# Loading and splitting the second half's up operands at other steps of the first half's down stage

## The chip, the cores and the metric

The kernel runs on one core of one Trainium2 chip. The metric is device time in microseconds (us) of one execution. The kernel before was timed in three runs; one further execution was recorded by the hardware profiler, and the trace comes from that one.

The engines are written as in the profile: PE (TensorE, matmuls; PEld its weight loads), DVE (VectorE), ACT (ScalarE), POOL (GpSimd) and SP (SyncE, which issues nearly all DMAs of this kernel). "SPq" is SyncE's issuing of transfers.

## The reference, cut to what matters

One decoder layer for 2048 tokens of width 1024, in f32: a token mixer of three groups of heads, then a channel mixer, then a final norm.

```python
D_MODEL = 1024; SEQ = 2048; DEPTH = 1
D_FF = 256 * ((8 * D_MODEL // 3 + 255) // 256)      # 2816

# channel mixer, in words of the reference's docstring:
#   Pre-RMSNorm with adaLN, then up-projection, causal depthwise conv (width 3),
#   SiLU-gated product, down-projection. Added to the residual with an adaLN gate.
# A final RMSNorm with gain is applied at the end.
```

The change lies in the channel mixer. Its up-projection (1024 to 2 x 2816) and its down-projection (2816 to 1024) are the two large matrix products behind the token mixer.

## The kernel before, in words

**Stages.** The token mixer comes first, in four blocks of 512 tokens. The channel mixer follows in two halves, s = 0 and s = 1, of 1024 tokens. Each half has an up stage and a down stage: up 0, down 0, up 1, down 1.

**How a product is computed.** Each large product is cut into 2 x 2 blocks and done with seven block products in place of eight (Strassen's scheme in Winograd's form); the products are numbered 1 to 7. Their operands are sums and differences of blocks. To keep f32 accuracy at the speed of a narrower type, every operand is split into a high and a low part: ScalarE casts the raw tile into the high part (L1186), VectorE subtracts that from the raw tile (L1187), and TensorE runs three matmuls per pair of operands: high x low and low x high around high x high (`split3`, L292 to L294). A split thus needs the raw tile in SBUF, then ScalarE, then VectorE, and TensorE waits for the second.

**The down stage** (L1633). The products run in the order TURN = 1, 2, 6, 7, 4, 5, 3. Each has 11 steps k, and each step has 12 matmuls of 128x512: four row tiles p, three matmuls each. Per step two raw tiles are loaded and split: `rd`, a weight block or a stored sum of weight blocks, into `dA`, and `rb`, an operand made from the up stage's outputs, into `dB`. Names are dA{half}_{product}_{step}. Products 1, 6, 7 and 4 add up in the same four PSUM banks `dX`; product 2 and product 5 have banks `dY`, and product 3 its own four banks, also called `dX`. After a product VectorE adds the banks, scaled by a gate, onto the residual rows `y` (L1672): the evacuation. Product 7's first matmuls wait until product 6 has been read out of the shared banks.

**Work woven into the down stage.** After each step of products 4, 5 and 3 the down stage calls `next(between)`, 33 calls in all. For the first half `between` is the generator `up_inputs(B)` (L1346), which prepares operands of the *second* half's up stage; each `yield` in it hands back to the down stage. It loads raw rows hr1_t_k (L1350) into a ring of three tiles (`t2m`, L1335) and works on them:

- Operands 1 and 2: the eight rows hr1_0_k "a" are loaded and split as they are.
- For k = 0 to 3 three "b" rows are loaded: b11 = hr1_0_k, b12 = hr1_1_k, b22 = hr1_1_(k+4). Three subtractions (L1360, L1363, L1367) make operands 5, 6 and 7 from them, each followed by a split into `B1_i_k` (in some tiles the high and low part are called `hB1`, `lB1`). After the second a copy of the difference is stored in DRAM (`t2d`, L1365), for `up_inputs_rest` (L1371), which makes operands 4 and 3 after the down stage.

In all that is 20 yields; what is left of the generator after the down stage would be run by the loop behind it.

**Behind it** come the weights for the second half's up stage: `up_weights` loads raw blocks and stored sums of blocks (`s`, loaded at L1401 into a ring of two tiles) and splits them into A1_f_i. The up stage's first matmuls also need the banks that product 3 used and a ScalarE copy `m` of an earlier result (L1474).

**What sets the order.** TensorE's order is written out by hand. The order on VectorE, ScalarE, SyncE and GpSimd is set by a scheduler when the program is built: it takes the instruction that is ready by its own estimate and has the highest priority. The down stage's loads and splits are raised by 60, its evacuations more; the generator's work is not raised. It is still put wherever the scheduler believes an engine free and the inputs there, which can be far ahead of the step at which it is written: the first "b" rows are written in product 4 and stand at the border between products 6 and 7. On the chip each engine then runs its list strictly in that order: an instruction that waits holds everything behind it on its engine. Two helpers touch the order: `marked(op)` (L251) remembers an instruction, and `pinned(fn)` (L255) issues what fn makes after the remembered one.

The order and reuse of tiles matter as well: a load into a ring's tile waits until the tile's last reader is done.

Of the kernel before, what the change touches and what calls it, by code (L numbers as in the profile page):

```python
# [14 lines left out]
ALU = mybir.AluOpType  # L15
# [109 lines left out]
def trunk(ctx, tc, xT, vecs, cvec, cst, rope, msk, wada, win, walow, wgla, wout, wup, wdown, out):  # L125
# [41 lines left out]
    V, S, G, T = nc.vector, nc.scalar, nc.gpsimd, nc.tensor  # L167
# [83 lines left out]
    def marked(op):  # L251

        mark[:] = [op.ins]

    def pinned(fn):  # L255

        with tc.issue_after(mark[0]):
            fn()
# [925 lines left out]
    def split(src, hi, lo):  # L1184

        S.copy(hi, src)  # L1186
        V.tensor_tensor(lo, src, hi, op=ALU.subtract)  # L1187
        return hi, lo

    def low_inputs(s, tile):  # L1190

        B = {}
        for i in (1, 2):
            for k in range(4):
                x = tile(f"hr{s}_{i}_{k}a")
                nc.sync.dma_start(x[:], h2d[2 * s, k + 4 * (i - 1)][:])
                B[i, k] = split(x[:], *hc_tile(f"B{s}_{i}_{k}"))
        return B

    def up_op(A, s, f, i, src):  # L1200
        t = w4_tile(f"A{s}_{f}_{i}")
        A[i] = split(src, t[:, 0:512], t[:, 512:1024])
# [45 lines left out]
    def split_made(B, i, raw):  # L1248
        for k, x in enumerate(raw):
            B[i, k] = split(x[:], *hc_tile(f"B0_{i}_{k}"))  # L1250
# [78 lines left out]
    def t2k(name):  # L1329
        return pg.tile([P, 512], F32, tag="t2k", name=name, bufs=4)  # L1330
# [4 lines left out]
    def t2m(name):  # L1335
        return pg.tile([P, 512], F32, tag="t2m", name=name, bufs=3)
# [6 lines left out]
    def up_op_in(B, i, k, src):  # L1343
        B[i, k] = split(src[:], *hc_tile(f"B1_{i}_{k}"))

    def up_inputs(B):  # L1346

        def raw(t, k, why):
            x = t2m(f"hr1_{t}_{k}{why}")
            nc.sync.dma_start(x[:], h2d[2 + t, k][:])  # L1350
            return x

        op = lambda i, k, src: up_op_in(B, i, k, src)
        for i in (1, 2):
            for k in range(4):
                op(i, k, raw(0, k + 4 * (i - 1), "a"))
                yield
        for k in range(4):
            b11, b12, b22 = raw(0, k, "b"), raw(1, k, "b"), raw(1, k + 4, "b")
            V.tensor_tensor(b11[:], b12[:], b11[:], op=ALU.subtract)  # L1360
            op(5, k, b11)
            yield
            V.tensor_tensor(b11[:], b22[:], b11[:], op=ALU.subtract)  # L1363
            op(6, k, b11)
            nc.sync.dma_start(t2d[k][:], b11[:])  # L1365
            yield
            V.tensor_tensor(b12[:], b22[:], b12[:], op=ALU.subtract)  # L1367
            op(7, k, b12)
            yield
# [325 lines left out]
    for k in range(4):  # L1695
        x = t2k(f"hr0_3_{k}")
# [5 lines left out]
    hc_room = R_H + R_T + R_A4 + R_HC  # L1702
    B = {}
    ahead = up_inputs(B)
    down_stage(0, ahead)
    A = up_weights(1, 0)
# [107 lines left out]
```

## Time and profile before

| | |
|---|---|
| three timed runs | 2415.09, 2420.59, 2421.57 us (median 2420.59) |
| the profiled execution | 2411.75 us, of which the span of the trace is 2410.0 |
| granted TensorE clock | 0.997 of full speed |
| DMA traffic | 525.78 MB, mean 218 GB/s over the span |
| first half's products 7, 4, 5 and 3 | 1636 to 1758 us of the span |
| one step of a product (12 matmuls) | 2.7 us |

The profile's page shows, for each engine, its busy time; then the chain of waits, followed back from the last instruction; then groups of instructions by line. Rows of the trace in order of time have the start in us, the duration, the engine, the line, the operation, output <- inputs and the shape; in square brackets stands the engine's idle time just before, and what ended it. Names are shown there without their numbers (`hr_0b` is hr1_0_0b, hr1_1_0b or hr1_1_4b), and several instructions in a row of one form are put together as "x3". A row of a transfer group has the median time from issue to landing at its end. A matmul is shown with 0.39 us where nothing holds it, but follows the one before by 0.23 us, since they are pipelined.

In a row of the view by stretches stand the stretch, its length, and for each engine (TensorE, its weight loads, VectorE, ScalarE, GpSimd, SyncE) the busy time and count of instructions in it; behind them the granted clock, the share in which the DMA engines were busy, and the GB/s that they moved.

### The profile page before, as it was taken

What the parts mean: (1) busy time and instruction counts of PE and PEld (TensorE: products, weight loads), DVE (VectorE), ACT (ScalarE), POOL (GpSimd) and SP (SyncE); (2) the same over time, 40 slices, a digit from 0 to 9 for tenths busy, and PEclk for the clock granted to TensorE, in tenths of its full rate; (3) what the DMA queues carried; (4) which work ended last, traced back from release to release, by engine and by line L of the source; (5) the groups of instructions that cost most, each with busy time, mean ns of one, the idle gap of its engine ahead of it and who ended that gap; (6) DMA issues with size and microseconds to landing.
All of it is one profiled execution on the core that took longest, in us unless ns stands there. A gap on an engine that the chain in (4) does not pass through costs nothing.

```text
span 2410.0 us, 51886 instructions
## 1 busy us (share of the span) xinstructions
PE 2365.0 (98%) x20523; PEld 1960.7 (81%) x20523; DVE 1817.1 (75%) x3391; ACT 1290.4 (54%) x2311; POOL 154.3 (6%) x275
## 2 busy tenths in 40 slices
PE   7999999999999999999999999999999999999998
PEld 5788878888788878887888888888878888888887
DVE  7687867868577746877988888866878787778566
ACT  4675456744665457644554454554455455555452
POOL 1000100000000100001000000000010100000000
PEclk9999999999999999999999999999999999999999
DMA  7655676897788857888554454686765444448663
GB/s 273 231 185 188 232 264 238 278 333 263 259 299 298 280 198 274 272 280 273 176 170 153 140 157 151 227 288 212 225 208 167 144 149 144 151 152 281 200 199 116
DMA packets 228885, 525.78 MB, mean 218 GB/s; under 512 B 25849, under 2 KB 28833, under 8 KB 228641
## 3 DMA queue, kind: packets, MB, share of 16 engines
q1 hardware_dynamic: 225440, 511.98, 63.7%
q0 software_dynamic: 3200, 10.49, 1.2%
q8 instruction: 161, 2.64, 0.4%
q14 instruction: 84, 0.68, 0.1%
HBM read 392.87 MB, written 129.50 MB: 217 GB/s over the span
## 4 chain that ended last, share of the span: by engine, by line
PE 77%; DVE 9%; DMA 6%; ACT 4%; issue 3%; SPq 0%; POOL 0%; DVEq 0%; ACTq 0%; POOLq 0%
PE X L292 6%; PE X L293 6%; PE X L294 6%; PE Z L293 3%; PE Z L294 3%; PE Z L292 3%; PE dX L292 3%; PE dX L294 3%; PE dX L293 3%; PE psqkvgr L292 3%; PE psqkvgr L294 2%; PE psqkvgr L293 2%; PE y L292 2%; PE y L293 2%; PE y L294 2%
## 5 line engine op out<-in xcount | busy, mean ns | idle before, releaser
L292 PE MATMUL X<-B,A 128*128 128x512 f32 x572 | 223.1, 390 | 0.7 <-ACT u L1490 0.7
L293 PE MATMUL X<-B,A 128*128 128x512 f32 x572 | 222.8, 390 | 0.3 <-DVE B L1187 0.3
L294 PE MATMUL X<-B,A 128*128 128x512 f32 x572 | 222.6, 389 | 0.0
L1187 DVE TENSOR_TENSOR dA<-rd,dA 128x512 fp32r<-128x512 f32 x154 | 106.0, 689 | 94.4 <-ACT dA L1186 93.9
L1186 ACT CAST dA<-rd 128x512 fp32r<-128x512 f32 x154 | 95.5, 621 | 149.3 <-PE dX L294 57.5
L292 PE MATMUL dX<-dB,dA 128*128 128x512 f32 x396 | 154.2, 389 | 1.0 <-DVE y L1672 1.0
L293 PE MATMUL dX<-dB,dA 128*128 128x512 f32 x396 | 154.2, 389 | 0.3 <-DVE dB L1187 0.3
L294 PE MATMUL dX<-dB,dA 128*128 128x512 f32 x396 | 154.1, 389 | 0.0
L1187 DVE TENSOR_TENSOR A<-s,A 128x512 fp32r<-128x512 f32 x176 | 120.5, 686 | 39.5 <-ACT A L1186 39.5
L1186 ACT CAST A<-s 128x512 fp32r<-128x512 f32 x176 | 108.5, 617 | 60.8 <-PE Z L294 41.9
L292 PE MATMUL psvgh<-hvgh,ha 128*128 128x256 f32 x480 | 139.6, 291 | 0.0
L293 PE MATMUL psvgh<-lvgh,ha 128*128 128x256 f32 x480 | 135.7, 283 | 0.0
L294 PE MATMUL psvgh<-hvgh,ha 128*128 128x256 f32 x480 | 135.7, 283 | 0.0
L292 PEld LDWEIGHTS X<-B,A 128*128 128x128 f32 x572 | 107.4, 188 | 23.9 <-ACT u L1490 1.7
L293 PEld LDWEIGHTS X<-B,A 128*128 128x128 f32 x572 | 107.4, 188 | 23.0 <-DVE B L1187 1.0
L294 PEld LDWEIGHTS X<-B,A 128*128 128x128 f32 x572 | 107.4, 188 | 22.3
L293 PE MATMUL Z<-B,A 128*128 128x512 f32 x308 | 120.5, 391 | 1.4 <-DVE B L1187 1.4
L292 PE MATMUL Z<-B,A 128*128 128x512 f32 x308 | 120.2, 390 | 0.3 <-ACT B L1186 0.2
L294 PE MATMUL Z<-B,A 128*128 128x512 f32 x308 | 119.9, 389 | 0.0
L1186 ACT CAST A<-r 128x512 fp32r<-128x512 f32 x132 | 82.3, 623 | 63.5 <-PE Z L294 60.0
L1187 DVE TENSOR_TENSOR A<-r,A 128x512 fp32r<-128x512 f32 x132 | 90.6, 687 | 30.3 <-ACT A L1186 29.9
L1187 DVE TENSOR_TENSOR dB<-rb,dB 128x512 fp32r<-128x512 f32 x154 | 105.4, 686 | 6.8 <-ACT dB L1186 6.8
(491 smaller groups left out, 6780.5 us busy)
## 6 DMA issues: line engine op xcount, KB each, us to landing
gs<-yv SPq DMA_DIRECT2D x154, 256.0 KB, 3.0
rb<-gs SPq DMA_DIRECT2D x154, 256.0 KB, 4.1
r<-wup SPq DMA_DIRECT2D x143, 256.0 KB, 3.4
s<-sumsu SPq DMA_DIRECT2D x132, 256.0 KB, 3.2
wada<-wada SPq DMA_DIRECT2D x48, 512.0 KB, 4.3
rd<-sumsd SPq DMA_DIRECT2D x88, 256.0 KB, 4.0
rd<-wdown SPq DMA_DIRECT2D x66, 256.0 KB, 4.0
x<-xT SPq DMA_DIRECT2D x64, 256.0 KB, 5.5
```

The source lines that it names most:

```text
L292: T.matmul(ps, lhs[0], rhs[0], start=first, stop=False, skip_group_check=more)
L293: T.matmul(ps, lhs[0], rhs[1], start=False, stop=False, skip_group_check=more)
L294: T.matmul(ps, lhs[1], rhs[0], start=False, stop=last, skip_group_check=more)
L1186: S.copy(hi, src)
L1187: V.tensor_tensor(lo, src, hi, op=ALU.subtract)
```

## The change

The generator `up_inputs` is written differently, and `split` marks its subtraction:

```diff
@@ -1184,7 +1184,7 @@
     def split(src, hi, lo):
 
         S.copy(hi, src)
-        V.tensor_tensor(lo, src, hi, op=ALU.subtract)
+        marked(V.tensor_tensor(lo, src, hi, op=ALU.subtract))
         return hi, lo
 
@@ -1353,11 +1353,14 @@
         op = lambda i, k, src: up_op_in(B, i, k, src)
         for i in (1, 2):
             for k in range(4):
-                op(i, k, raw(0, k + 4 * (i - 1), "a"))
+                x = raw(0, k + 4 * (i - 1), "a")
                 yield
+                op(i, k, x)
         for k in range(4):
             b11, b12, b22 = raw(0, k, "b"), raw(1, k, "b"), raw(1, k + 4, "b")
-            V.tensor_tensor(b11[:], b12[:], b11[:], op=ALU.subtract)
+            yield
+            yield
+            pinned(lambda: V.tensor_tensor(b11[:], b12[:], b11[:], op=ALU.subtract))
             op(5, k, b11)
             yield
             V.tensor_tensor(b11[:], b22[:], b11[:], op=ALU.subtract)
```

An "a" row is loaded, the down stage runs one step, and then the row is split. The three "b" rows of a k are loaded, two steps pass, and only then the first subtraction is written, tied behind the last marked one (the split that the down stage wrote last). The generator now has 28 yields; there are still 33 calls. Lines below it have moved by three.

The loads and matmuls are the same, and so is the arithmetic. TensorE's order does not change; on the other engines the built order differs in 42 rows (VectorE), 22 (ScalarE), 16 (SyncE) and 8 (GpSimd). The eight "a" rows move nowhere. Three places show the rest.

VectorE at the border between the first half's products 6 and 7, before:

```order
L1187 TENSOR_TENSOR dA0_7_5_20507<-rd0_7_5_20505,dA0_7_5_20507 128x512
L1187 TENSOR_TENSOR dB0_7_5_20512<-rb0_7_5_20510,dB0_7_5_20512 128x512
L1360 TENSOR_TENSOR hr1_0_0b_20879<-hr1_1_0b_20881,hr1_0_0b_20879 128x512
L1187 TENSOR_TENSOR lB1_5_0_20887<-hr1_0_0b_20879,hB1_5_0_20886 128x512
L1672 SCALAR_TENSOR_TENSOR y0_1_0_19865<-dX0_0_19612,mod_102,y0_1_0_19865 128x512
L1672 SCALAR_TENSOR_TENSOR y0_1_0_19865<-dX0_1_19613,mod_102,y0_1_0_19865 128x512
L1672 SCALAR_TENSOR_TENSOR y0_1_2_19866<-dX0_2_19614,mod_102,y0_1_2_19866 128x512
L1672 SCALAR_TENSOR_TENSOR y0_1_2_19866<-dX0_3_19615,mod_102,y0_1_2_19866 128x512
L1187 TENSOR_TENSOR dA0_7_6_20529<-rd0_7_6_20527,dA0_7_6_20529 128x512
```

and in the changed kernel:

```order
L1187 TENSOR_TENSOR dA0_7_5_20507<-rd0_7_5_20505,dA0_7_5_20507 128x512
L1187 TENSOR_TENSOR dB0_7_5_20512<-rb0_7_5_20510,dB0_7_5_20512 128x512
L1187 TENSOR_TENSOR dA0_7_6_20529<-rd0_7_6_20527,dA0_7_6_20529 128x512
L1675 SCALAR_TENSOR_TENSOR y0_1_0_19865<-dX0_0_19612,mod_102,y0_1_0_19865 128x512
L1675 SCALAR_TENSOR_TENSOR y0_1_0_19865<-dX0_1_19613,mod_102,y0_1_0_19865 128x512
L1675 SCALAR_TENSOR_TENSOR y0_1_2_19866<-dX0_2_19614,mod_102,y0_1_2_19866 128x512
L1675 SCALAR_TENSOR_TENSOR y0_1_2_19866<-dX0_3_19615,mod_102,y0_1_2_19866 128x512
L1187 TENSOR_TENSOR dB0_7_6_20534<-rb0_7_6_20532,dB0_7_6_20534 128x512
```

The first subtraction for k = 0 and the split of its result stood ahead of the evacuation of product 6; now one split of a weight for product 7 stands there. The other four operations of k = 0 came after the evacuation and are gone from there too.

VectorE between the first half's products 4 and 5, in the changed kernel; this is where k = 0 stands now:

```order
L1187 TENSOR_TENSOR dB0_4_10_20914<-rb0_4_10_20912,dB0_4_10_20914 128x512
L1363 TENSOR_TENSOR hr1_0_0b_20879<-hr1_1_0b_20881,hr1_0_0b_20879 128x512
L1370 TENSOR_TENSOR hr1_1_0b_20881<-hr1_1_4b_20883,hr1_1_0b_20881 128x512
L1187 TENSOR_TENSOR lB1_5_0_20931<-hr1_0_0b_20879,hB1_5_0_20930 128x512
L1187 TENSOR_TENSOR dA0_5_0_20957<-rd0_5_0_20955,dA0_5_0_20957 128x512
L1187 TENSOR_TENSOR dB0_5_0_20962<-rb0_5_0_20960,dB0_5_0_20962 128x512
L1366 TENSOR_TENSOR hr1_0_0b_20879<-hr1_1_4b_20883,hr1_0_0b_20879 128x512
L1187 TENSOR_TENSOR dA0_5_1_20985<-rd0_5_1_20983,dA0_5_1_20985 128x512
```

Before, dA and dB of product 5's step 0 followed dB0_4_10 directly. The loads of the three rows stay where they were in SyncE's list, at the border between products 6 and 7; the store of the difference (L1365 before, L1368 now) goes 28 operand loads later.

VectorE in product 3, the last of the first half, before (n3a and sqn3 are sums of squares for the final norm):

```order
L1363 TENSOR_TENSOR hr1_0_3b_21190<-hr1_1_7b_21194,hr1_0_3b_21190 128x512
L1533 SCALAR_TENSOR_TENSOR y0_0_2_19861<-y0_0_2_19861,vec2_15933,n3b0_0_20961 128x512
L1187 TENSOR_TENSOR dA0_3_5_21453<-rd0_3_5_21451,dA0_3_5_21453 128x512
L391 TENSOR_TENSOR n3a0_1_19617<-n3a0_1_19617,sqn3_0_1_5_21322 128x512
L1187 TENSOR_TENSOR B1_6_3_21231<-hr1_0_3b_21190,B1_6_3_21231 128x512
L1187 TENSOR_TENSOR B1_7_3_21260<-hr1_1_3b_21192,B1_7_3_21260 128x512
L391 TENSOR_TENSOR n3a0_1_19617<-n3a0_1_19617,sqn3_0_1_6_21325 128x512
L1187 TENSOR_TENSOR dB0_3_5_21458<-rb0_3_5_21456,dB0_3_5_21458 128x512
```

and where k = 3 stands in the changed kernel:

```order
L1187 TENSOR_TENSOR dB0_3_7_21502<-rb0_3_7_21500,dB0_3_7_21502 128x512
L1363 TENSOR_TENSOR hr1_0_3b_21366<-hr1_1_3b_21368,hr1_0_3b_21366 128x512
L1187 TENSOR_TENSOR dA0_3_8_21519<-rd0_3_8_21517,dA0_3_8_21519 128x512
L1187 TENSOR_TENSOR dB0_3_8_21524<-rb0_3_8_21522,dB0_3_8_21524 128x512
L1187 TENSOR_TENSOR B1_5_3_21417<-hr1_0_3b_21366,B1_5_3_21417 128x512
L1187 TENSOR_TENSOR dA0_3_9_21541<-rd0_3_9_21539,dA0_3_9_21541 128x512
L1187 TENSOR_TENSOR dB0_3_9_21546<-rb0_3_9_21544,dB0_3_9_21546 128x512
L1366 TENSOR_TENSOR hr1_0_3b_21366<-hr1_1_7b_21370,hr1_0_3b_21366 128x512
L1187 TENSOR_TENSOR dA0_3_10_21563<-rd0_3_10_21561,dA0_3_10_21563 128x512
L1187 TENSOR_TENSOR dB0_3_10_21568<-rb0_3_10_21566,dB0_3_10_21568 128x512
L1187 TENSOR_TENSOR B1_6_3_21443<-hr1_0_3b_21366,B1_6_3_21443 128x512
L1370 TENSOR_TENSOR hr1_1_3b_21368<-hr1_1_7b_21370,hr1_1_3b_21368 128x512
```

The six operations of k = 3 stood ahead of dB0_3_5 (step 5); now they begin behind dB0_3_7, and the last (the split B1_7_3) comes three rows after these, between the first splits A1_0_i of the second half's weights. In SyncE's list the loads of k = 3 move too. Before:

```order
L1365 DMA t2d2_15906<-hr1_0_2b_21105 128x512
L1350 DMA hr1_0_3b_21190<-h2d2_3_173 128x512
L1340 DMA rd0_3_7_21495<-sumsd7_11127 128x512
L1350 DMA hr1_1_3b_21192<-h2d3_3_181 128x512
L1350 DMA hr1_1_7b_21194<-h2d3_7_185 128x512
L1658 DMA rb0_3_7_21500<-gs0_3_7_215 128x512
```

and in the changed kernel:

```order
L1661 DMA rb0_3_8_21522<-gs0_3_8_216 128x512
L1350 DMA hr1_0_3b_21366<-h2d2_3_173 128x512
L1340 DMA rd0_3_9_21539<-sumsd9_13912 128x512
L1350 DMA hr1_1_3b_21368<-h2d3_3_181 128x512
L1661 DMA rb0_3_9_21544<-gs0_3_9_217 128x512
L1350 DMA hr1_1_7b_21370<-h2d3_7_185 128x512
L1340 DMA rd0_3_10_21561<-sumsd10_14966 128x512
```

They stood at the loads of step 7 and stand now at those of steps 8 to 10. The rows of k = 1 and k = 2 keep their place in SyncE's list; on VectorE k = 1 keeps its order, and k = 2 mixes differently with four splits.

## The prediction

> **What bounds the kernel now.** I read the page's engine shares first, then the chain of waits, then each engine's rows in time order for the stretch that the change touches.
>
> ```profile
> PE 2365.0 (98%) x20523; PEld 1960.7 (81%) x20523; DVE 1817.1 (75%) x3391; ACT 1290.4 (54%) x2311; POOL 154.3 (6%) x275
> PE 77%; DVE 9%; DMA 6%; ACT 4%; issue 3%; SPq 0%; POOL 0%; DVEq 0%; ACTq 0%; POOLq 0%
> ```
>
> TensorE is busy for 98% of the span and carries 77% of the chain. A change that leaves its matmuls alone can only open or close gaps between them, so the question is which gaps lie where the change works: the last products of the first half's down stage and the first products of the second half's up stage. The largest is at the border between down products 6 and 7 (each row gives start, duration, instruction, and in brackets the idle time before it and what ended it):
>
> ```profile
> 1634.96 0.39 PE L294 MATMUL dX<-dB,dA 128*128 128x512 f32 x1
> 1636.38 0.47 PE L292 MATMUL dX<-dB,dA 128*128 128x512 f32 x1 [1.03 <-DVE y L1672]
> 1636.68 0.40 PE L293 MATMUL dX<-dB,dA 128*128 128x512 f32 x1
> ...
> 1666.18 0.39 PE L294 MATMUL dX<-dB,dA 128*128 128x512 f32 x1
> 1666.41 0.39 PE L292 MATMUL dX<-dB,dA 128*128 128x512 f32 x1
> ```
>
> Unhindered, matmuls start 0.23 us apart, as at the next border (7 to 4, 1666.18 to 1666.41). At the border 6 to 7 it is 1636.38 - 1634.96 = 1.42, and 0.30 for the next one: 1.19 + 0.07, about 1.26 us lost. Product 7 adds onto the banks of product 6, so it waits until VectorE has taken product 6 out of them (L1672). That evacuation was late:
>
> ```profile
> 1631.21 0.69 DVE L1187 TENSOR_TENSOR dB<-rb,dB 128x512 fp32r<-128x512 f32 x1
> 1633.50 0.69 DVE L1360 TENSOR_TENSOR hr_0b<-hr_0b,hr_0b 128x512 f32<-128x512 f32 x1 [1.59 <-DMA hr_0b<-h2d]
> 1634.88 0.69 DVE L1187 TENSOR_TENSOR lB<-hr_0b,hB 128x512 fp32r<-128x512 f32 x1 [0.69 <-ACT hB L1186]
> 1635.48 2.06 DVE L1672 SCALAR_TENSOR_TENSOR y<-dX,mod,y 128x512 f32<-128x512 f32 x3
> ...
> 1665.15 2.72 DVE L1672 SCALAR_TENSOR_TENSOR y<-dX,mod,y 128x512 f32<-128x512 f32 x4
> ```
>
> VectorE stood 1.59 us at the first subtraction for the second half (L1360) until its rows had landed, then 0.69 us for ScalarE's cast, and only then evacuated, from 1635.48. At the next border, with no such work in its queue, it began at 1665.15, 1.26 us ahead of the matmul that needs it. The two rows were asked for shortly before:
>
> ```profile
> 1627.57 0.90 SPq L1350 DMA_DIRECT2D hr_0b<-h2d  x2
> ...
> hr_0b<-h2d SPq DMA_DIRECT2D x2, 256.0 KB, 5.2
> ```
>
> Issued from 1627.57, they took 5.2 us to land; VectorE was free at 1631.9.
>
> **The change part by part.** *The eight rows of operands 1 and 2:* the text loads them one step earlier, but in the built order neither their transfers nor their splits move on any engine. 0 us.
>
> *Row k = 0.* Its subtraction and split leave the place ahead of the evacuation and go behind the split of product 4's last operand; its loads stay. Ahead of the evacuation now stands one weight split of product 7 (dA of step 6), whose cast needs a buffer that TensorE frees once per step:
>
> ```profile
> 1627.27 0.62 ACT L1186 CAST dA<-rd 128x512 fp32r<-128x512 f32 x1
> 1629.95 0.62 ACT L1186 CAST dA<-rd 128x512 fp32r<-128x512 f32 x1 [0.57 <-PE dX L294]
> 1634.22 0.62 ACT L1186 CAST hB<-hr_0b 128x512 fp32r<-128x512 f32 x1 [3.13 <-DVE hr_0b L1360]
> ```
>
> The rhythm is 2.7 us, so without the 3.13 us wait the next cast falls at 1632.7, its subtraction at 1633.3 to 1634.0, and the evacuation has read the first bank by 1634.7; TensorE wants that bank at 1634.96 + 0.23 = 1635.2. The gap closes with 0.5 us to spare. **-1.26 us.**
>
> The Trainium skill, SBUF — State Buffer, section The DMA setup-cost knee, fits a transfer by 2 us plus its bytes at 436 GB/s, an estimate of 2.6 us for 256 KB; by it the rows would have been down before VectorE was free, there would be no wait of 1.59 us, and this term would be near 0 (rival 3 has the chance of that); the row has 5.2, twice as much.
>
> At the new place VectorE has this room:
>
> ```profile
> 1676.03 0.69 DVE L1187 TENSOR_TENSOR dB<-rb,dB 128x512 fp32r<-128x512 f32 x1
> 1678.14 0.69 DVE L1187 TENSOR_TENSOR dA<-rd,dA 128x512 fp32r<-128x512 f32 x1 [1.42 <-ACT dA L1186]
> 1680.86 0.69 DVE L1187 TENSOR_TENSOR dA<-rd,dA 128x512 fp32r<-128x512 f32 x1 [1.43 <-ACT dA L1186]
> ```
>
> Six operations of k = 0 (three subtractions, three splits, 0.6 us apart) are 3.6 us against 1.4 us idle in each 2.7 us step: absorbed in three steps. Their rows landed 40 us before. What queues behind them is splits for product 5, which TensorE reaches 30 us after 1666.41, at 1696: 18 us of cover for at most 3.6 us of lateness, and 3.6 us would be the price without it. The three casts go to ScalarE, which waits for TensorE's buffers there. The store of the difference moves 28 operand loads back in SP's queue and is read only in the second half. 0 us.
>
> *Rows k = 1 and 2* keep their loads' place in SP's queue; k = 1 keeps its order on VectorE, k = 2 only mixes differently with four splits. 0 us.
>
> *Row k = 3* can go either way. In product 3 VectorE has little lead, and one split comes late:
>
> ```profile
> 1727.07 0.69 DVE L1360 TENSOR_TENSOR hr_3b<-hr_3b,hr_3b 128x512 f32<-128x512 f32 x1 [1.53 <-DMA hr_3b<-h2d]
> 1738.89 0.69 DVE L391 TENSOR_TENSOR n3a<-n3a,sqn 128x512 f32<-128x512 f32 x1 [1.59 <-ACT sqn L390]
> 1741.31 0.68 DVE L1187 TENSOR_TENSOR dB<-rb,dB 128x512 fp32r<-128x512 f32 x1
> ...
> 1737.09 0.62 ACT L1186 CAST dA<-rd 128x512 fp32r<-128x512 f32 x1 [3.90 <-DMA rd<-sumsd]
> ...
> 1741.37 0.39 PE L292 MATMUL dX<-dB,dA 128*128 128x512 f32 x1
> 1742.05 0.50 PE L293 MATMUL dX<-dB,dA 128*128 128x512 f32 x1 [0.29 <-DVE dB L1187]
> ```
>
> TensorE loses 0.68 - 0.23 = 0.45 us and about 0.11 in the restart, 0.56. In the new order the six operations of k = 3 and the 1.53 us wait leave the place ahead of this dB (step 5) and stand behind step 7. What still holds dB is ScalarE, which must pass the cast at 1737.09 (3.90 us on a transfer) before the square that VectorE adds first. So I put dB at about 1738.4, 3 us in time. **-0.56 us.**
>
> Late next is the same work, now between product 3 and the second half's first weights:
>
> ```profile
> 1750.77 0.69 DVE L1187 TENSOR_TENSOR A<-r,A 128x512 fp32r<-128x512 f32 x1 [0.59 <-ACT A L1186]
> 1751.81 0.69 DVE L1187 TENSOR_TENSOR A<-r,A 128x512 fp32r<-128x512 f32 x1 [0.35 <-ACT A L1186]
> 1752.42 1.29 DVE L1187 TENSOR_TENSOR A<-s,A 128x512 fp32r<-128x512 f32 x2
> 1757.68 0.69 DVE L1187 TENSOR_TENSOR A<-s,A 128x512 fp32r<-128x512 f32 x1 [3.97 <-ACT A L1186]
> ...
> 1753.13 5.59 SPq L1401 DMA_DIRECT2D s<-sumsu  x3
> ```
>
> The splits of the first two weight sums (1752.42 to 1753.7) free the buffers for the next sums (SP, 1753.13), on which VectorE then waits 3.97 us. Product 3's evacuation, its squares and ScalarE's copy of m stand behind, and TensorE waits for that copy (second row below; the first is product 3's last matmul): from those splits on, a delay passes on one to one. VectorE's work from 1725 to 1754 is the same in both orders; its idle time in it was 1.53 + 1.59 + 0.59 and small change, some 4 us, and with a wait for the square and one for a cast I expect 3 to 4. So I take the splits as on time: 0 us. Both ends are kept: above, six waits in the second half's first 40 us name ScalarE or VectorE.
>
> ```profile
> 1758.09 0.39 PE L294 MATMUL dX<-dB,dA 128*128 128x512 f32 x1
> 1764.21 0.50 PE L292 MATMUL X<-hB,A 128*128 128x512 f32 x1 [0.29 <-ACT m L1474]
> 1776.43 0.50 PE L292 MATMUL X<-B,A 128*128 128x512 f32 x1 [0.16 <-ACT u L1490]
> 1781.06 0.50 PE L293 MATMUL Z<-B,A 128*128 128x512 f32 x1 [0.22 <-DVE B L1187]
> 1782.36 0.50 PE L293 MATMUL Z<-B,A 128*128 128x512 f32 x1 [0.23 <-DVE B L1187]
> 1783.97 0.50 PE L293 MATMUL Z<-B,A 128*128 128x512 f32 x1 [0.31 <-DVE B L1187]
> 1794.15 0.50 PE L292 MATMUL X<-hB,A 128*128 128x512 f32 x1 [0.43 <-ACT u L1486]
> ```
>
> Their idle time is 1.64 us; each also loses 0.39 - 0.23 that the modelled end hides and 0.11 in the restart, 6 x 0.27 = 1.6: at most -3.3 us if all six close. Below: one landing of 5.2 us in front of those splits, less the idle 0.59 and 0.35 ahead of the A splits, +4.3.
>
> **Sum.** -1.26 - 0.56 = -1.8 us. Against the profiled execution, 2411.75 us (its span is 2410.0), that is 2409.9. The three runs shown are 2415.09, 2420.59 and 2421.57, with the profiled one four executions of one program; the middle of the four is 2417.8 (2.8 below the median of three), and I forecast **2416.0**.
>
> **The rivals.** (1) *The lead carries over:* everything in front of the second half comes earlier and its six waits close too. For it: VectorE's idle time in product 3 is all waiting on others. Against: the sums' loads still take their 4 us, and VectorE is full afterwards. -1.8 - 3.3 = -5.1, 2412.7.
>
> (2) *Row k = 3 becomes the new wait, slower than before:* its loads now stand in SP's queue behind operand loads of product 3 that wait for splits, and its second subtraction stands ahead of dA of step 10. If the row is still in the air there, VectorE stands a whole landing with the second half's first weights behind it, and the copy of m is that late. For it: the 1.53 us wait at 1727.07 and 5.2 us per landing. Against: its last load is released by dB of step 5, so by the estimate above it goes out near 1739 and has until about 1745. -1.26 + 4.3 = +3.0, 2420.8; slower from a wait of about 2.2 us on (1.26 plus the idle 0.94). The Trainium skill, TensorE: Matmul & The Clock Gate, section What's actually happening, has the array at half clock after an idle window of about 3.4 us, for about as long again; a gap of 4.3 us would then cost an estimated 1.7 us more, 2422.5; no gap in the rows above is long enough to show it.
>
> (3) *The gap at 1634.96 is worth nothing:* the profiled execution caught a slow landing, and where the rows land within 1631.9 - 1628.0 = 3.9 us there is no wait to remove.
>
> ```profile
> s<-sumsu SPq DMA_DIRECT2D x132, 256.0 KB, 3.2
> ...
> 1626.00:1634.00 8.00, 8.00 (x37) 6.63 (x36) 5.60 (x9) 3.82 (x7) 0.00 (x0) 1.00 0.89 300
> ```
>
> For it: the same size lands in 3.2 us in the median of another group. Against: around the subtraction the DMA engines are busy for 0.89 of the time (the last but one number), from loads that are in the program in every execution. 2417.8 - 0.56 = 2417.2. The fit of the Trainium skill named above would have it so.
>
> **How the numbers follow.** Forecast 0.62, rival 1 0.15, rival 2 0.13, rival 3 0.10. The forecast's own spread is from -3.5 to -0.5 us, and single runs scatter by 6.1 below and 3.7 above their middle. The range takes rival 1 with part of the scatter below, and above rival 2's price with most of the scatter: 2409 to 2424. What a measurement can tell from no change is 0.3%, 7.3 us; no case reaches that alone, so faster or slower by more is left to scatter on top of a case: faster 0.09 (rival 1 and part of the forecast), slower 0.04 (rival 2), same 0.87.
>
> **What would show it.** Right: in the changed profile the first matmul of product 7 starts 0.23 us after the last of product 6; the k = 0 subtraction near 1675 has no DMA wait before it; the wait on dB in product 3 is gone. Wrong: a wait at the border on L1672's successor; a DMA wait of over 2 us before a k = 3 subtraction near 1745; a copy of m that ends later than 6.1 us after product 3's last matmul starts (1764.2 against 1758.1 now). The forecast as a whole is wrong if TensorE's busy time changes, or if its idle time before 1634 does.

## The result and the profile after

| | before | changed |
|---|---|---|
| median of 20 runs | 2418.57 us (2415.09 to 2424.21) | 2414.26 us (2409.44 to 2417.50) |
| profiled execution | 2411.75, span 2410.0 | 2409.44, span 2407.7 |

The ratio of changed to before is 0.9985, 95% interval [0.9979, 0.9991]: -3.6 us, between -5.1 and -2.2. The forecast was 2416.0 and -1.8 us. Time and direction fit, and the gain is about twice the sum that was made.

The profiled pair gives -2.3 us of span. The changed kernel's page, engine shares and chain of waits:

```profile
PE 2364.9 (98%) x20523; PEld 1961.5 (81%) x20523; DVE 1818.2 (76%) x3391; ACT 1292.1 (54%) x2311; POOL 153.9 (6%) x275
PE 82%; DVE 8%; DMA 5%; ACT 4%; issue 1%; SPq 0%; DVEq 0%; POOL 0%; ACTq 0%
```

TensorE's busy time is the same within 0.1 us, so what went is idle time between its matmuls; its share of the chain rose from 77 to 82%. At the border between products 6 and 7 (VectorE first, then TensorE):

```profile
1633.72 0.69 DVE L1187 TENSOR_TENSOR dA<-rd,dA 128x512 fp32r<-128x512 f32 x1 [0.72 <-ACT dA L1186]
1634.33 2.06 DVE L1675 SCALAR_TENSOR_TENSOR y<-dX,mod,y 128x512 f32<-128x512 f32 x3
...
1635.36 0.39 PE L294 MATMUL dX<-dB,dA 128*128 128x512 f32 x1
1635.59 0.39 PE L292 MATMUL dX<-dB,dA 128*128 128x512 f32 x1
```

The evacuation starts at 1634.33 and needs about 0.69 for the first bank, which TensorE takes at 1635.59: 0.57 us to spare, and the first matmul of product 7 starts 0.23 us after the last of product 6. At the new place, behind the last operand split of product 4, the rows of k = 0 have long landed:

```profile
1675.13 0.69 DVE L1187 TENSOR_TENSOR dB<-rb,dB 128x512 fp32r<-128x512 f32 x1
1675.73 0.69 DVE L1363 TENSOR_TENSOR hr_0b<-hr_0b,hr_0b 128x512 f32<-128x512 f32 x1
...
1681.22 1.29 DVE L1187 TENSOR_TENSOR lB<-hr_0b,hB 128x512 fp32r<-128x512 f32 x2
...
1685.44 0.69 DVE L1187 TENSOR_TENSOR dA<-rd,dA 128x512 fp32r<-128x512 f32 x1 [1.42 <-ACT dA L1186]
```

No bracket stands at the subtraction; the six operations are done by 1682.5, and from 1685.44 VectorE idles 1.42 us a step again.

In product 3, and on to the second half's first weights:

```profile
1736.15 0.68 DVE L1187 TENSOR_TENSOR dB<-rb,dB 128x512 fp32r<-128x512 f32 x1
...
1741.52 0.69 DVE L1363 TENSOR_TENSOR hr_3b<-hr_3b,hr_3b 128x512 f32<-128x512 f32 x1 [0.94 <-DMA hr_3b<-h2d]
...
1745.14 0.69 DVE L1366 TENSOR_TENSOR hr_3b<-hr_7b,hr_3b 128x512 f32<-128x512 f32 x1
...
1750.29 1.29 DVE L1187 TENSOR_TENSOR A<-s,A 128x512 fp32r<-128x512 f32 x2
1755.41 0.69 DVE L1187 TENSOR_TENSOR A<-s,A 128x512 fp32r<-128x512 f32 x1 [3.83 <-ACT A L1186]
...
1757.22 2.72 DVE L1675 SCALAR_TENSOR_TENSOR y<-dX,mod,y 128x512 f32<-128x512 f32 x4
```

dB of step 5 is the first row. Row k = 3 waits 0.94 us on its first load and not at all on its last. TensorE's waits by cause, all of those listed between 1600 and 1820 in the changed kernel:

```profile
PE Z L293 <- DVE B L1187: 0.8, 3, 0.3
PE X L292 <- ACT u L1489: 0.5, 1, 0.5
```

The waits on y, on dB and on the copy of m, which stood in the prediction's rows, are gone in this trace.

**Three stretches.** Since TensorE's order is the same in all kernels here, the starts of three matmuls cut each profiled execution in comparable pieces: the first of the down stage (s = 0), the first of its product 5, and the first of the second half. In the changed kernel's first trace, for example, the last of these is the first row here, and in the kernel before's the second:

```profile
1756.79 0.39 PE L292 MATMUL X<-B,A 128*128 128x512 f32 x1
```

```profile
1758.32 0.39 PE L292 MATMUL X<-B,A 128*128 128x512 f32 x1
```

In the best executions the three lie 149.60 and 61.36 us apart. What an execution has above that is lost at the border (first piece) or in product 3 (second). The third piece runs to the end of the span. The kernels with a part alone are explained below.

| execution | border | product 3 | second half to the end | down stage to the end |
|---|---|---|---|---|
| before | 1.30 | 0.63 | 651.67 | 864.56 |
| before, second | 0.65 | 0.40 | 656.42 | 868.43 |
| before, third | 0.53 | 0 | 654.87 | 866.36 |
| k = 0 alone | 0 | 0 | 652.05 | 863.01 |
| k = 0 alone, second | 0 | 2.09 | 654.30 | 867.35 |
| k = 2, 3 alone | 3.73 | 0 | 650.99 | 865.69 |
| k = 2, 3 alone, second | 1.69 | 0 | 653.30 | 865.95 |
| changed | 0 | 0 | 650.89 | 861.85 |
| changed, second | 0 | 0 | 652.95 | 863.91 |
| changed, third | 0 | 0 | 654.91 | 865.87 |

The kernel before averages 866.45 and the changed one 863.88, -2.6 us. What comes ahead of the down stage ended at 1545.43, 1551.04 and 1548.73 us in the three executions of before: much of the scatter of the times lies where the change does nothing.

The third piece has a scatter of its own that the table doesn't name. In five of the ten executions TensorE's granted clock fell to 0.5 for 3 to 7 us between 1787 and 1799, in five it stayed at 1.00 there. One of the first kind (before, second) and one of the second kind (before):

```profile
1792.00:1796.00 4.00, 4.00 (x9) 2.89 (x10) 4.00 (x7) 1.88 (x4) 1.62 (x3) 0.50 0.29 98
```

```profile
1788.00:1792.00 4.00, 4.00 (x20) 3.30 (x19) 3.61 (x6) 1.75 (x2) 1.79 (x4) 1.00 0.89 309
```

TensorE is busy throughout in both, with 9 matmuls in 4 us against 20. The five with the slow stretch (before, second and third; k = 0 alone, second; k = 2, 3 alone, second; changed, third) are the five with the longest third piece, 653.30 to 656.42; the others have 650.89 to 652.95.

### The profile page after: what moved, and what is told of

Its sections match the earlier page's. It is cut to its first block, busy times and chain, and to the rows that moved or that the text cites. A ratio compares the mean times of both kernels' runs of the same rounds, so it can differ in the third digit from the quotient of the medians.

```text
span 2407.7 us, 51890 instructions
## 1 busy us (share of the span) xinstructions
PE 2364.9 (98%) x20523; PEld 1961.5 (81%) x20523; DVE 1818.2 (76%) x3391; ACT 1292.1 (54%) x2311; POOL 153.9 (6%) x275
## 4 chain that ended last, share of the span: by engine, by line
PE 82%; DVE 8%; DMA 5%; ACT 4%; issue 1%; SPq 0%; DVEq 0%; POOL 0%; ACTq 0%
PE X L292 6%; PE X L294 6%; PE X L293 6%; PE dX L292 4%; PE dX L293 4%; PE dX L294 4%; PE Z L293 3%; PE Z L294 3%; PE Z L292 3%; PE psqkvgr L292 3%; PE psqkvgr L294 2%; PE psqkvgr L293 2%; PE y L292 2%; PE y L293 2%; PE y L294 2%; PE dY L292 2%
```

## The experiments

**What the parts move.** In the built order, the tie has an effect only at k = 0, and the extra steps only at k = 2 and 3. The loads of the "a" rows one step ahead change nothing by themselves, nor does the tie without the steps. So two kernels take the change apart cleanly, and the changed kernel is both together.

**The part for k = 0 alone** (run twice):

```diff
-            yield
-            yield
-            pinned(lambda: V.tensor_tensor(b11[:], b12[:], b11[:], op=ALU.subtract))
+            if k == 0:
+                yield
+                yield
+                pinned(lambda: V.tensor_tensor(b11[:], b12[:], b11[:], op=ALU.subtract))
+            else:
+                V.tensor_tensor(b11[:], b12[:], b11[:], op=ALU.subtract)
```

> The two steps and the tie for k = 0 alone; k = 1 to 3 as before. The built order differs from the kernel before only in the work of k = 0. Theory: the border's 1.26 us go and nothing else changes: -1.3 us (ratio 0.9995). Rival (ordinary executions lose more at this border than the profiled one, and that is the whole gain measured): -3 us or more (0.9988 or less). Rival (the moved work is a load in product 5): 0 or slower.

> The part for k = 0 alone, a second execution. Theory: no gap at the border; dB in product 3 may stop TensorE for up to 0.56 us and the copy of m for up to 1.4 us, as in the kernel before, since row k = 3 stands at its old place; from the down stage to the end 863 to 866 us; -0.5 to -1.5 us against the kernel before. Rival (this part is the whole gain): as low as the changed kernel, 862 to 864 us, -3 us.

Measured: 0.9997 [0.9989, 1.0006] and 0.9997 [0.9987, 1.0006], some -0.7 us both times. The border has no gap in either. From the down stage to the end the second execution took 867.35 us, more than either side expected. Its product 3 shows what row k = 3 does at its old place (VectorE, then TensorE):

```profile
1734.05 0.69 DVE L1366 TENSOR_TENSOR hr_3b<-hr_3b,hr_3b 128x512 f32<-128x512 f32 x1 [3.16 <-DMA hr_3b<-h2d]
...
1744.81 1.28 DVE L1187 TENSOR_TENSOR B<-hr_3b,B 128x512 fp32r<-128x512 f32 x2
1746.01 0.68 DVE L391 TENSOR_TENSOR n3a<-n3a,sqn 128x512 f32<-128x512 f32 x1
1746.61 0.68 DVE L1187 TENSOR_TENSOR dB<-rb,dB 128x512 fp32r<-128x512 f32 x1
...
1745.16 0.39 PE L292 MATMUL dX<-dB,dA 128*128 128x512 f32 x1
1747.35 0.50 PE L293 MATMUL dX<-dB,dA 128*128 128x512 f32 x1 [1.80 <-DVE dB L1187]
```

VectorE waits 3.16 us for the row, is then busy without a break, and the splits of row k = 3 stand ahead of dB. TensorE stands from 1745.16 to 1747.35: the 0.56 us of the first trace is 2.09 here. No trace without the work of k = 0 at the border has its gap, but a gain of 0.5 to 1.3 us is less than these timed runs tell from nothing, and they don't show it.

**The part for k = 2 and 3 alone** (run twice): the steps without the tie.

```diff
             yield
             yield
-            pinned(lambda: V.tensor_tensor(b11[:], b12[:], b11[:], op=ALU.subtract))
+            V.tensor_tensor(b11[:], b12[:], b11[:], op=ALU.subtract)
```

> The rows one step and two steps ahead, but the first subtraction not tied. The built order is that of the changed kernel, except that the work of k = 0 stands at the border again as before. Theory: the gap at the border stays (1.2 to 1.6 us), the wait on dB in product 3 (0.56) and the one on ScalarE's copy of m (0.56) are gone: -1.0 us (ratio 0.9996). Rival (the row k = 3 gives nothing by itself): 0. Rival (the untimed rest of the measured -3.6 us is here): -2.3 us (0.9990).

> The part for k = 2 and 3 alone, a second execution. Theory: a gap of 0.5 to 4 us at the border as in the kernel before; no gap on dB in product 3 and under 0.3 us at the copy of m; from there to the end 651 to 653 us as in the changed kernel, against 651.7 to 656.4 in the kernel before; -2 us. Rival (this part gives nothing): a gap at the copy of m, 653 us or more from there to the end.

Measured: 0.9985 [0.9976, 0.9994] and 0.9987 [0.9978, 0.9996], -3.6 and -3.1 us, clear of no change both times and more than the -1 and -2 us expected. Product 3 has no gap, and none stands at the copy of m. The border's gap is back, and in the first execution larger than ever:

```profile
1632.29 0.69 DVE L1187 TENSOR_TENSOR dB<-rb,dB 128x512 fp32r<-128x512 f32 x1
1635.08 0.69 DVE L1363 TENSOR_TENSOR hr_0b<-hr_0b,hr_0b 128x512 f32<-128x512 f32 x1 [2.11 <-DMA hr_0b<-h2d]
1636.46 0.69 DVE L1187 TENSOR_TENSOR lB<-hr_0b,hB 128x512 fp32r<-128x512 f32 x1 [0.69 <-ACT hB L1186]
...
1635.72 0.39 PE L294 MATMUL dX<-dB,dA 128*128 128x512 f32 x1
1637.96 0.56 PE L292 MATMUL dX<-dB,dA 128*128 128x512 f32 x1 [1.85 <-DVE y L1675]
1638.32 0.63 PE L293 MATMUL dX<-dB,dA 128*128 128x512 f32 x1
1638.75 0.63 PE L294 MATMUL dX<-dB,dA 128*128 128x512 f32 x1
```

The rows landed 2.11 us after VectorE was free; the gap is 2.24 - 0.23 = 2.0 us, and another 1.7 is lost since the following matmuls are 0.43 us apart in place of 0.23 (under the last heading below).

**The same kernels again.**

> The kernel before, unchanged, once more: a second profiled execution of it. Theory (the gap at the border between products 6 and 7 is a late landing that every execution has): the first matmul of product 7 again starts 1.2 to 1.6 us after the last of product 6, the first subtraction waits 1.3 to 2.0 us on its rows, and dB in product 3 again stops TensorE for about 0.5 us; ratio to itself 1.000 within 0.06%. Rival (one slow landing was caught): the gap is under 0.5 us here.

> The kernel before, a third profiled execution and more timed runs. Theory (the border's gap is a landing time and differs from execution to execution): between 0.5 and 4 us at the border, and 5 to 11 us in the second half's start; the mean of the gaps from 1600 to 1850 over the profiled executions is 3 to 4 us above that of the changed kernel. Rival (the gaps do not carry the measured difference): within 1 us of the changed kernel's.

> The changed kernel, unchanged, beside the others on the same chip. Theory: -2.3 us as the two profiles show (0.9990), the sum of the two parts; if the parts add up and the rest of -3.6 is in one of them, that one shows it: 0.9985. Its profile has no gap at the border and none on dB in product 3.

> The changed kernel, a third profiled execution and more timed runs. Theory: no gap at the border, none on dB in product 3, under 0.3 us at the copy of m; from the first half's down stage to the end 862 to 864 us, against 864.6, 868.4 and 866.4 in the three executions of the kernel before; 2414. Rival (the two executions so far were lucky): 865 us or more.

Measured: the kernel before against itself 0.9996 [0.9988, 1.0005] and 0.9996 [0.9985, 1.0008]; the changed one 0.9991 [0.9983, 1.0000] and 0.9985 [0.9977, 0.9994]. So 0.04% either way means nothing here. The changed kernel's three ratios give 2 to 4 us; the interval of the second of them reaches 1.0000, and the kernel before as it ran beside it had a median of 2415.21 against 2414.04. At the border the second and the third execution of before have:

```profile
1638.45 0.69 DVE L1360 TENSOR_TENSOR hr_0b<-hr_0b,hr_0b 128x512 f32<-128x512 f32 x1 [0.94 <-DMA hr_0b<-h2d]
...
1641.34 0.47 PE L292 MATMUL dX<-dB,dA 128*128 128x512 f32 x1 [0.37 <-DVE y L1672]
```

```profile
1636.04 0.69 DVE L1360 TENSOR_TENSOR hr_0b<-hr_0b,hr_0b 128x512 f32<-128x512 f32 x1 [0.70 <-DMA hr_0b<-h2d]
...
1638.92 0.47 PE L292 MATMUL dX<-dB,dA 128*128 128x512 f32 x1 [0.27 <-DVE y L1672]
```

The second execution came out between what was expected: product 7 starts 0.76 us after product 6, not 1.2 to 1.6, but 0.65 us is lost, not under 0.5. The gap varies with the landing, but was there in all five executions that have the work at the border. From the down stage to the end the means differ by 2.6 us, where 3 to 4 were expected. The third execution of the changed kernel came out as its rival said, 865.87 us: its loss at the second half's start is as large as in the kernel before (654.91 from there to the end), with the copy of m 1.06 us late and the clock at half for a while.

**What a delay ahead of the second half costs.** Six extra VectorE operations on the first weight sum, result unchanged:

```diff
                     nc.sync.dma_start(t[:], sums["u", f][:, j, :])
+                    for _ in range(6 if (s, f, i) == (1, 0, 6) else 0):
+                        V.tensor_tensor(t[:], t[:], t[:], op=ALU.max)
                     op(i, t[:])
```

> The changed kernel with six extra VectorE operations (maximum of a tile with itself, 0.60 us apart, the result unchanged) on the raw weight sum just ahead of the split A1_0_6, the first of the two A <- s splits behind product 3; nothing else in the built order moves. They stand in for a late landing of row k = 3. Theory (a delay of these splits passes on one to one to TensorE, through the buffers of the sums and the copy of m): the splits come 3.6 to 4.2 us later, and the gap ahead of the second half's first matmul that needs the copy of m grows from 0 to 3 to 4 us: +3 to +4 us, 2417 to 2418.5. Rival (VectorE's wait of 3.8 us for the next sums takes it up): no gap there, 0 to +0.5 us.

Measured: 2417.64 us, 0.9997 [0.9987, 1.0008], 0.06 to 0.12% above the changed kernel's ratios.

```profile
1754.37 0.69 DVE L1187 TENSOR_TENSOR A<-s,A 128x512 fp32r<-128x512 f32 x1
1754.97 2.86 DVE L1406 TENSOR_TENSOR s<-s 128x512 f32<-128x512 f32 x4
1758.76 1.29 DVE L1187 TENSOR_TENSOR A<-s,A 128x512 fp32r<-128x512 f32 x2 [0.93 <-ACT A L1186]
...
1763.76 0.69 DVE L1187 TENSOR_TENSOR A<-s,A 128x512 fp32r<-128x512 f32 x1 [3.10 <-ACT A L1186]
1764.36 2.72 DVE L1677 SCALAR_TENSOR_TENSOR y<-dX,mod,y 128x512 f32<-128x512 f32 x4
...
1766.60 0.39 PE L294 MATMUL Y<-B,A 128*128 128x512 f32 x1
1768.38 0.50 PE L292 MATMUL X<-hB,A 128*128 128x512 f32 x1 [1.39 <-ACT m L1479]
```

The order moved more than was expected. The split A1_0_5, which stood behind A1_0_6, now stands between the six operations (1754.37) and frees its buffer as early as ever; A1_0_7, which uses that buffer, now stands ahead of A1_0_6 (the pair from 1758.76). So one of the two splits was delayed and not both: a late row k = 3 would hold both. Against the second half's first matmul (1761.39 here, 1756.79 in the first trace of the changed kernel) A1_0_6, the second of the pair, comes at about -2.0 in place of -6.5, 4.5 us later. The last split of a sum, A1_0_3, and the evacuation behind it come at 2.4 and 3.0; in the changed kernel the evacuation came at 0.4, 1.4 and 2.5. TensorE's gap ahead of the copy of m is 1.78 - 0.23 = 1.55, against 0, 0 and 1.06. So the rival's "nothing" falls; the theory's "one to one" is not what this trace shows either (4.5 us at the split, 2.6 at the evacuation, 1.55 at TensorE, against the first trace), but for a delay of both splits it stays untested. Over the executions of this table the gap is the evacuation's lateness less 1.4 us, and none below that.

| execution | evacuation after the second half's first matmul | gap at the copy of m |
|---|---|---|
| changed; k = 2, 3 alone | 0.43, 1.39, 2.48; 0.74, -0.71 | 0, 0, 1.06; 0, 0 |
| before; k = 0 alone | 1.88, 2.77, 1.78; 1.37, 2.47 | 0.45, 1.34, 0.36; 0, 1.05 |
| delayed splits | 2.98 | 1.55 |

**Three attempts on the loss at the second half's start.** There TensorE waits for the splits of operands 4 and 3, whose raw rows (`hr_t`, `hr_b`) come late: their ring t2k is held by the four squares of product 3. First, all four squares in the other ring:

```diff
-                        sumsq(accs[h], y[h, m + p], ..., room=t2k if i == 3 else None)
+                        sumsq(accs[h], y[h, m + p], ..., room=None)
```

> The changed kernel, with the four squares of product 3 kept in the ring of three tiles that the rows used (t2m) in place of the ring of the operand loads (t2k). The loads for operands 4 and 3 of the second half then needn't wait until VectorE has added the squares: in SyncE's list they stand 11 rows earlier, and their splits earlier on VectorE. Theory (the 5 to 11 us that TensorE loses in the second half's first weight block, 1770 to 1840, come from the late landing of these rows): most of the Z <- B waits go, -3 to -5 us against the changed kernel, about 2409 to 2411. Rival (the rows now stand ahead of the weight sums and of product 3's evacuation, and these become late): the copy of m waits again, 0 to +3 us.

Second, the rows of operand 4 in the other ring:

```diff
-            t2, b21 = t2k(f"hr1_t2_{k}"), t2k(f"hr1_b21_{k}")
+            t2, b21 = t2m(f"hr1_t2_{k}"), t2m(f"hr1_b21_{k}")
```

> The changed kernel, with the raw rows of operand 4 (both loads) in the ring t2m, squares as they were. The first pair is loaded 7 and 6 rows earlier in SyncE's list, later pairs a little earlier. Theory (the late rows are the cause): about half of the loss at the second half's start goes, -1 to -3 us. Rival (the first X copies, which share that ring, wait for these rows): 0 to +2 us.

Measured: 2414.32 us, 0.9988 [0.9977, 1.0000], and 2419.36 us, 1.0006 [0.9997, 1.0016]. The first:

```profile
1757.74 0.69 DVE L1379 TENSOR_TENSOR hr_b<-hr_b,hr_t 128x512 f32<-128x512 f32 x1 [1.47 <-DMA hr_b<-h2d]
1758.35 0.68 DVE L1187 TENSOR_TENSOR A<-r,A 128x512 fp32r<-128x512 f32 x1
...
1760.39 0.69 DVE L1379 TENSOR_TENSOR hr_b<-hr_b,hr_t 128x512 f32<-128x512 f32 x1 [0.57 <-DMA hr_b<-h2d]
...
1761.60 2.72 DVE L1675 SCALAR_TENSOR_TENSOR y<-dX,mod,y 128x512 f32<-128x512 f32 x4
...
1768.39 0.80 PE L292 MATMUL X<-hB,A 128*128 128x512 f32 x1 [4.79 <-ACT m L1477]
```

The waits for operands 4 and 3 are gone, as the theory said, but the rows now stand, waiting for transfers, ahead of the evacuation. The evacuation is 3.6 us behind the second half's first matmul, the copy of m also needs a tile of the ring that the squares fill, and TensorE stands 4.79 us. In the second kernel the evacuation comes at 4.8 and the gap is 7.6 us, of which 4.8 - 1.4 explains less than half. The row of the copy shows the rest:

```profile
1772.69 0.59 ACT L1477 COPY m<-X 128x512 f32<-128x512 f32 x1 [1.27 <-DVE B L1187]
```

ScalarE waited for VectorE's split of a row of operand 4 (B), which frees a tile of the ring that m needs. Both rivals named the right mechanism, the second at too low a price: it is the fault of the border between 6 and 7 once more, put in at another place.

Third, two squares in each ring, so that the first pair of rows needs no square and the copy of m has a tile, and the rows stay behind the evacuation:

```diff
-                        sumsq(accs[h], y[h, m + p], ..., room=t2k if i == 3 else None)
+                        sumsq(accs[h], y[h, m + p], ..., room=t2k if i == 3 and p > 1 else None)
```

> The changed kernel with two of product 3's four squares in the ring t2m and two in t2k. The first pair of rows for operand 4 no longer waits for a square; the third tile of t2m stays free for the copy of m. Nothing is put ahead of product 3's evacuation on VectorE. Theory (the rows' landing sets the loss at the second half's start, and moving them ahead of the evacuation is what spoilt the two kernels that tried): no gap at the copy of m, the loss from 1770 to 1840 falls by 1 to 2 us, 2412 to 2413. Rival (later pairs still wait for squares, and the last pair decides): no change, 2414.

Measured: **2412.08 us**, 0.9979 [0.9968, 0.9990] (8 runs); the changed kernel in the same session 2414.56, 0.9985. The first pair's loads go out at 1757.25 and 1757.72:

```profile
1757.25 0.42 SPq L1377 DMA_DIRECT2D hr_t<-t2d  x1
1757.72 0.42 SPq L1378 DMA_DIRECT2D hr_b<-h2d  x1
```

That is 0.5 us ahead of the second half's first matmul (1757.74); in the changed kernel it was 3.8 behind (1760.57 to 1756.79). No gap stands at the copy of m, and 650.53 us from the second half's first matmul to the end is less than in any other execution. But TensorE still stands 1.94 us for a split of operand 4 or 3 (Z <- B, at 1782.44), where the three executions of the changed kernel stood 0.3, 2.1 and 1.2 us at most: that the rows' landing no longer costs is not shown, and the rival (later pairs still wait) is not excluded. It is faster than the kernel before; that it beats the changed kernel, by some 2 us, is not shown: the intervals overlap, and there is one trace.

## Why the prediction was right, and where its sum was short

**The border, -1.26: right in cause; the size is one draw of a scattered thing.** All five executions with the work of k = 0 at the border lost time there (1.30, 0.65, 0.53, 3.73, 1.69, mean 1.6), all five without it, and four further kernels without it, lost none. That 1.26 lies near the mean is luck: the three executions of the kernel before alone have a mean of 0.8, and the timed runs of this part show -0.7 us, not told from nothing. The cast's rhythm, the place of the freed split and the half microsecond to spare came out as worked out from the trace.

**dB of product 3, -0.56: right in cause, and again one draw of a scattered size.** The five executions with row k = 3 at its old place lost 0.63, 0.40, 0, 0 and 2.09 (mean 0.6), the five at the new place none. In the first trace dB comes 20.6 us ahead of the second half's first matmul (1736.15 to 1756.79), against 17.0 before (1741.31 to 1758.32): 3.6 us earlier, where 3 were forecast.

**Row k = 3 at its new place, 0 with bounds from -3.3 to +4.3: the term that looks too small.** The first pair of traces has -0.8 there (651.67 to 650.89), most of it the gap at the copy of m (0.45 and a slow restart). The means of five executions at the old place (653.9) and five at the new one (652.6) differ by 1.2 us, so the forecast of 0 looks short in the direction of rival 1. With single executions spread over 4 to 5 us on either side, this mean is a hint and no proof, and part of it may be the clock: three of the five at the old place and two of the five at the new one had the stretch at half clock. Among those at full clock the old place has 651.67 and 652.05, the new one 650.89, 650.99 and 652.95. But the timed runs of this part alone (0.9985, 0.9987) ask for more than the 0.6 us of product 3. The three means, 1.6 + 0.6 + 1.2 = 3.4 us, come near the measured 3.6; the timed parts divide it otherwise, some 0.7 for k = 0 and 3.1 to 3.6 for the rest, with intervals of about 2 us on either side. So it stays open where the gain beyond the forecast lies, and whether the new place makes the slow stretch rarer. The first A <- s splits do not come earlier on average (6.1 us before the second half's first matmul at the old place, 6.2 at the new one), which is what the forecast took; the evacuation does (2.1 us behind it at the old place, 0.9 at the new one).

The step "from those splits on, a delay passes on one to one" left out slack: an evacuation up to 1.4 us behind the second half's first matmul made no gap in any execution, and only what is beyond 1.4 us came through one to one. Ahead of the evacuation, 4.5 us of delay in one of the two splits became 2.6. Rival 2's price of 4.3 us left out that slack: in the first trace, with the evacuation at 0.43, the first 1.0 us would have cost nothing. Its wait on the last load did not come in any trace (0.3 to 0.95 us on the first subtraction of row k = 3, none on the second and third).

Two of the signs that were to show the forecast wrong did come. TensorE's down stage begins 0.40 us later in the changed profile (1545.43 to 1545.83), and in the third execution of the changed kernel the matmul behind the copy of m starts 6.7 us after product 3's last matmul (6.1 was the limit). Both lie within what executions of one kernel differ by, so as signs they were too sharp.

**Rival 3, the gap worth nothing: refuted by the landings.** The group of these two loads took 5.2, 4.9, 4.6, 5.4 and 4.4 us to land in the five executions, never 3.9, and VectorE waited for them in each (1.59, 0.94, 0.70, 2.11 and 0.83 us).

The transfer rule cited there, the Trainium skill's SBUF — State Buffer, section The DMA setup-cost knee, an estimate of 2.6 us for 256 KB, is 1.8 to 2.8 us short of these five.

**The level.** The forecast sits between the single profiled time and the three runs; twenty runs put the kernel before at 2418.57, 0.8 above the middle that was taken. The stretch ahead of the change alone differs by 5.6 us between executions. With twenty runs on each side the interval came to 1.5 us either way, so the 0.3% that the prediction took for the least that can be told was too coarse.

## What to carry to other kernels

What an instruction that must wait for a transfer costs depends on what stands behind it on its engine: put it behind the evacuation or the split that TensorE waits for next, even if its rows are then in SBUF for 40 us. Read that from the rows ahead of a gap on the engine that is late, and count the ring that a moved load or square occupies. For an effect of 0.1%, cut several traces at the same matmuls and compare the pieces, with the granted clock of each: the pieces show what the total's scatter hides.

## What was not expected of the hardware

After a gap the matmuls can go on at half the rate. The view by stretches, for the kernel with k = 2 and 3 alone behind its 1.85 us of idle time at the border, and for the one with all squares moved behind 4.79 us (the last three numbers are the granted clock, the DMA share and GB/s):

```profile
1638.00:1642.00 4.00, 4.00 (x11) 3.13 (x12) 4.00 (x7) 0.51 (x1) 0.00 (x0) 0.57 0.08 27
```

```profile
1768.00:1772.00 4.00, 3.61 (x9) 2.84 (x9) 3.58 (x6) 1.47 (x3) 0.00 (x0) 0.50 0.49 151
```

The granted clock was 0.57 and 0.50. But the second execution of the changed kernel idled 2.14 us, longer than the first of these, and kept its clock:

```profile
1785.65 0.50 PE L292 MATMUL Z<-B,A 128*128 128x512 f32 x1 [2.14 <-ACT B L1186]
...
1786.00:1790.00 4.00, 3.77 (x17) 3.01 (x17) 4.00 (x7) 1.71 (x4) 1.76 (x4) 1.00 0.32 105
```

So the length of one gap does not decide it, and a gap of some 2 us cost 2 us here and nearly 4 there. The prediction said that no gap in its rows was long enough to show this; the border's gap was, in another execution. The Trainium skill, TensorE: Matmul & The Clock Gate, section What's actually happening, has a free-running window of about 3.4 us after which the clock is halved or restored. A window that runs freely fits gaps of 1.85 and 2.14 us with opposite outcomes, and the slow stretch of the first (1637.96 to about 1641.7) is near its 3.4 us; that the window must be wholly idle, as the prediction had taken it, does not agree with the 1.85 us.
